# Layer 1's in-projection by Strassen's seven block products, and output projection 0 as one stage with its weights resident

## The chip, the core and the metric

The kernel runs on one core of one Trainium2 chip. The metric is the time of one launch on the device, in microseconds, by the median of several runs. The core has a matrix engine (TensorE, here PE) and three engines that work element by element: VectorE (DVE), ScalarE (ACT) and GpSimd (POOL). SyncE (SP) issues the DMAs. Tiles lie in SBUF, 128 partitions wide; matmuls write to PSUM, from which ACT and DVE read.

## What is computed

Two layers of a small diffusion backbone, over 2176 tokens (128 of a prompt, 2048 latent), 1024 channels, float32. Layer 0 mixes with gated linear attention and a spatial gate, layer 1 with centred pooling means and a short gated convolution. The change is in layer 1's input projection (`h @ w_in_odd`, 1024 to 3072 channels) and in the order and the blocks of layer 0's output projection:

```python
def mix_odd(z, j):
    B, T, _ = z.shape
    xc, gc, xd, bd, cd, gd = split_cols(z, ODD_SPLITS)
    pooled = jnp.concatenate(
        [centred_mean(xc[..., i * DG_C:(i + 1) * DG_C], w) for i, w in enumerate(POOL_WINDOWS)],
        axis=-1) - xc
    pooled = jnp.einsum('btgc,gcd->btgd', pooled.reshape(B, T, G_C, DG_C), w_pool[j])
    o_c = pooled.reshape(B, T, BRANCH_W) * pool_scale[j] * jax.nn.silu(gc)
    u = cd * xd
    up = jnp.pad(u, ((0, 0), (1, 1), (0, 0)))
    y = up[:, :-2] * w_conv[j, 0] + up[:, 1:-1] * w_conv[j, 1] + up[:, 2:] * w_conv[j, 2]
    o_d = bd * y * jax.nn.silu(gd)
    return jnp.concatenate([o_c, o_d], axis=-1)
...
for l in range(DEPTH):
    h = rmsnorm(x, norm_g[l]) * (1.0 + scale) + shift
    ...
    out = out @ w_out[l]
    x = x + gate * out
return rmsnorm(x, final_norm_g), finals
```

## The kernel before

**Products.** Channels lie on partitions, tokens along the free dimension. Every large float32 product is made of three fp32r matmuls: both operands are split in a rounded part `hi` and a rest `lo`, and hi x hi, hi x lo and lo x hi are summed in PSUM (`mm3`, L212). `split` (L197) makes `hi` by a copy on ACT and `lo = src - hi` by a subtraction on DVE or, every third time, on POOL (`lo_engine`, L193). `gemm_ch` (L220) makes one tile of 128 output channels: it loads 128x1024 weights with `load_w` (L204; three `hi`/`lo` pairs in the pool `wp`), splits them, and for each group of at most 512 tokens issues 8 x 3 matmuls.

**Stages.** Layer 0's in-projection and mixing run to about 854 us, in blocks of 512 and 640 tokens. Then come four token blocks of 544 (`BLK2`), each with three stages: output projection 0 (`out0`, L975, through `out_proj`, L955), layer 1's in-projection and mixing (`in1`, L1002), output projection 1 with the final norm (`out1`, L1116, and `out1_last`, L1140, for the last block). The order is written out by hand in the last lines of the kernel: out0(3), out0(2), in1(3), out1(3), out0(1), in1(2), out1(2), out0(0), in1(1), out1(1), in1(0), out1(0). So the output projection 0 of a block runs one stage ahead of the in1 that needs it.

**in1.** It loads the residual stream `x1` and the row `r` of reciprocal norms from DRAM, makes the normed operand `h` for eight channel tiles (`make_t`, L348, on DVE; `make_h`, L359: `hi` on ACT, `lo` on DVE), and for each of four heads `hh` runs six `gemm_ch` calls (cd, xd, gate of D, xc, gate of C, bd), each in two groups of 268 to 276 tokens. The results are consumed from PSUM by ACT copies, DVE products and `silu_psum` (L277); pooling steps are additions on POOL (L1082).

**Side work.** Smaller work is cut into generators that `tick` (L143) advances once per `gemm_ch`. `finish_o` (L837) is such work: per tile of 128 tokens it combines the attention halves, norms them (`newton`) and splits the eight `o` tiles that `out0` reads. `finish_rstd` sums squares over the channels by matmuls with ones (L248, L249) and finishes 1/sqrt by Newton steps on ACT and DVE (L240 to L261). The code is scheduled by the framework: instructions of one engine run in the order it settles on, which may put an instruction ahead of one that the code issues earlier.

## Time and profile before

| quantity | value |
|---|---|
| median of 3 runs | 1907.23 us (1899.83 to 1910.7) |
| profiled execution, its own time | 1902.82 us |
| its span in the profile | 1901.0 us |
| mean granted TensorE clock | 0.979 |
| PE busy | 1801.7 us (95%), 16303 matmuls |
| DVE, ACT, POOL busy | 60%, 45%, 38% |

The span is the profiled execution from its first to its last recorded instruction. Busy time is the union of an engine's instructions; matmuls overlap in the engine, so the mean duration of one (290 ns) is not what it takes from the stream: that is the distance from one start to the next. A duration on DVE and POOL includes whatever the instruction waited after it had started. The name `ps_g L217` stands for any product of `mm3`; `L199` for any `lo` part, `L198` for any `hi` part.

### The profile page before, as it was taken

To read this page: it belongs to the slowest core of one execution; us is meant where nothing else is said; L and a number is where in the kernel's file an instruction comes from. 1 tells how busy PE (TensorE), PEld (TensorE's weight loads), DVE (VectorE), ACT (ScalarE), POOL (GpSimd) and SP (SyncE) were. 2 spreads that over 40 slices of the span, in tenths; PEclk is the share of its full clock that TensorE was granted. 3 is DMA by queue.
4 is the path that set the end of the run, shared out by engine and by line. 5 is a ranking of instruction groups with operands and counts; after the bars stand their busy time and mean duration, and the time that the engine had idled before them with its cause. 6 is when DMAs were issued, how large, how long until landed. Compare 5 with 4: busy or idle time off the path is not lost. (4 is left out here: it accounts for less than half of the span.)

```text
span 1901.0 us, 40150 instructions
## 1 busy us (share of the span) xinstructions
PE 1801.7 (95%) x16303; PEld 1678.6 (88%) x16303; DVE 1149.6 (60%) x2069; ACT 857.3 (45%) x1678; POOL 730.5 (38%) x707
## 2 busy tenths in 40 slices
...
GB/s 310 117 123 152 153 102 136 128 159 113 140 126 102 114 106 94 142 172 183 245 200 157 109 146 109 246 157 96 95 130 203 196 81 87 115 141 130 80 89 60
DMA packets 136121, 263.43 MB, mean 139 GB/s; under 512 B 24192, under 2 KB 60160, under 8 KB 135936
## 3 DMA queue, kind: packets, MB, share of 16 engines
...
q8 instruction: 128, 2.10, 0.5%
q14 instruction: 57, 0.47, 0.1%
...
## 5 line engine op out<-in xcount | busy, mean ns | idle before, releaser
L217 PE MATMUL ps_g<-ring_hh,wp_hi 128*128 128x272 f32 (+5 forms) x2168 | 679.1, 314 | 4.4 <-ACT ring_hh L365 2.7
L217 PE MATMUL ps_g<-ring_hl,wp_hi 128*128 128x272 f32 (+5 forms) x2168 | 672.4, 310 | 1.1 <-DVE ring_hl L366 1.0
L217 PE MATMUL ps_g<-ring_hh,wp_lo 128*128 128x272 f32 (+5 forms) x2168 | 673.1, 311 | 0.0
L198 ACT ACTIVATE wp_hi<-wp_raw 128x1024 fp32r<-128x1024 f32 (+1 forms) x256 | 271.1, 1059 | 435.5 <-PE ps_g L217 323.5
L217 PEld LDWEIGHTS ps_g<-ring_hh,wp_hi 128*128 128x128 f32 x2168 | 409.6, 189 | 27.6 <-issue 3.8
L217 PEld LDWEIGHTS ps_g<-ring_hl,wp_hi 128*128 128x128 f32 x2168 | 410.0, 189 | 18.4 <-DVE ring_hl L366 2.0
L217 PEld LDWEIGHTS ps_g<-ring_hh,wp_lo 128*128 128x128 f32 x2168 | 409.1, 189 | 16.4 <-issue 0.7
L199 DVE TENSOR_TENSOR wp_lo<-wp_raw,wp_hi 128x1024 fp32r<-128x1024 f32 (+1 forms) x174 | 226.7, 1303 | 201.2 <-ACT wp_hi L198 200.9
L199 POOL TENSOR_TENSOR wp_lo<-wp_raw,wp_hi 128x1024 fp32r<-128x1024 f32 (+1 forms) x82 | 201.1, 2452 | 362.1 <-ACT wp_hi L198 359.5
L270 POOL TENSOR_TENSOR tmp_acc<-tmp_acc,tmp_px 128x544 f32<-128x544 f32 (+4 forms) x76 | 120.4, 1584 | 160.6 <-ACT tmp_px L269 155.2
L217 PE MATMUL ps_g<-wp_hi,ring_hh 128*128 128x256 f32 (+1 forms) x528 | 157.4, 300 | 7.9 <-ACT gl_v L700 4.4
L217 PE MATMUL ps_g<-oA_oh,wp_hi 128*128 128x272 f32 (+1 forms) x512 | 149.0, 295 | 7.1 <-ACT oA_oh L198 4.0
L524 POOL TENSOR_TENSOR gl_Z<-gl_Z 128x128 f32<-128x128 f32 x170 | 91.9, 561 | 161.8 <-DVE gl_Z L524 110.6
L217 PE MATMUL ps_g<-wp_hi,ring_hl 128*128 128x256 f32 (+1 forms) x528 | 152.4, 291 | 0.5 <-DVE ring_hl L366 0.4
L217 PE MATMUL ps_g<-wp_lo,ring_hh 128*128 128x256 f32 (+1 forms) x528 | 152.6, 291 | 0.2 <-POOL wp_lo L199 0.2
L217 PE MATMUL ps_g<-oA_ol,wp_hi 128*128 128x272 f32 (+1 forms) x512 | 150.0, 294 | 2.2 <-DVE oA_ol L199 2.0
L217 PE MATMUL ps_g<-oA_oh,wp_lo 128*128 128x272 f32 (+1 forms) x512 | 149.8, 294 | 0.1
L217 PE MATMUL ps_g<-oB_oh,wp_hi 128*128 128x272 f32 (+1 forms) x512 | 147.2, 289 | 0.7 <-ACT oB_oh L198 0.7
L217 PE MATMUL ps_g<-oB_oh,wp_lo 128*128 128x272 f32 (+1 forms) x512 | 147.5, 289 | 0.0
L217 PE MATMUL ps_g<-oB_ol,wp_hi 128*128 128x272 f32 (+1 forms) x512 | 147.3, 288 | 0.0
L286 POOL TENSOR_TENSOR tmp_ev<-tmp_ev,tmp_ev 128x272 f32<-128x272 f32 (+5 forms) x52 | 51.7, 994 | 186.4 <-ACT tmp_ev L275 176.7
L508 ACT ACTIVATE gl_L<-gl_Z 128x256 f32<-128x256 f32 x204 | 81.9, 417 | 87.3 <-DVE gl_Z L524 65.5
...
## 6 DMA issues: line engine op xcount, KB each, us to landing
...
xs_y<-in_xT_dram SPq DMA_DIRECT2D x32, 272.0 KB, 3.7
dr_x<-xs_y SPq DMA_DIRECT2D x32, 272.0 KB, 3.4
...
```

Of the source, the lines that this page charges most:

```text
L198: act(out=hi, in_=src, func=AF.Copy)
L199: (eng or lo_engine()).tensor_tensor(out=lo, in0=src, in1=hi.bitcast(F32), op=ALU.subtract)
L217: mm(out=out, lhsT=a, rhs=b, start=start and i == 0, stop=stop and i == n - 1)
L270: eng.tensor_tensor(out=acc, in0=acc, in1=sq, op=ALU.add)
L286: eng.tensor_tensor(out=x, in0=x, in1=s, op=ALU.mult)
L508: act(out=dst.rearrange("p (b t s) -> p t b s", t=2, s=s), in_=diag_ap(Z, 2 * i, s), func=AF.Exp, scale=1.0 / 16.0)
L524: (dve if i >= 2 or s < 4 else gps).tensor_tensor(out=dst, in0=dst, in1=bc(src), op=ALU.add)
```

## The change

**Output projection 0 as one stage.** It works in five blocks of its own (`BLKO`: 512, 512, 512, 384 and 256 tokens, from the end), one group per channel tile. Its eight weight tiles are split once, in the first block, and kept (three in `wp`, five in a new pool `wr`). While block i is multiplied, `finish_o` of block i+1 is ticked along. All five blocks run ahead of layer 1; the last `finish_rstd` is called at once, and the pools of this part are closed before layer 1's are opened in their place.

**In-projection by pairs.** The 24 output tiles of a block form 12 pairs, and the 8 channel tiles are halved into 4 + 4, the tokens into two parts of 272 or 280 columns. With A the weights of a pair (2 x 2 blocks) and B the operand (2 x 2 blocks), each pair takes seven products instead of eight: A11 B11, A12 B21, S1 T1, S2 T2, S3 T3, A22 T4, S4 B22, where S1 to S4 are sums of weight blocks and T1 to T4 sums of operand blocks. Several products add up in the same PSUM bank; ACT copies intermediate sums out (`copy`), and DVE makes the final sums (`plus`). `operand` prepares for each of four k the seven B matrices in `hi` and `lo`, on DVE, POOL and ACT. Weights are now loaded in halves of 128x512 (7 raw, 5 `hi` and 5 `lo` buffers); POOL takes three `lo` parts of seven. Block 3, which comes first, makes S1 to S4 (two additions each on POOL and DVE) and stores them in DRAM; blocks 2, 1 and 0 load them.

**Output projection 1** is as before, in weight halves, with two early parts placed at the end of in1 (`fill`).

```diff
+BLKO = [(1664, 2176), (1152, 1664), (640, 1152), (256, 640), (0, 256)]
+NBO = len(BLKO)
...
+    def w_out0(c):
+        if c == len(wres):
+            if c < NHI:
+                wres.append(load_w(wo[0, c], KT * P))
+            else:
+                raw = raw_tile()[:, 0:KT * P]
+                load(out=raw, in_=wo[0, c])
+                hi, lo = (wr.tile([P, KT * P], F32R, tag=f"{z}{c}") for z in "hl")
+                split(raw, hi, lo)
+                wres.append((hi, lo))
...
+    for i in range(NBO):
+        f = fin_o(i + 1, 1) if i + 1 < NBO else None
+        out0(i, of)
+        of = f() if f else None
+    drain()
+    s2.close()
+    late.close()
+    sw.close()
...
+    def split_half(raw):
+
+        half_ctr[0] += 1
+        hi, lo = (wh.tile([P, 512], F32R, tag=z, bufs=5) for z in ("hi", "lo"))
+        split(raw, hi, lo, gps if half_ctr[0] % 7 in (1, 3, 5) else dve)
+        return hi, lo
...
+        def sums(self):
+            R = self.raw
+            for i, (a, b, op, eng) in enumerate((("A21", "A22", ALU.add, gps),
+                                                 ("S1", "A11", ALU.subtract, dve),
+                                                 ("A11", "A21", ALU.subtract, gps),
+                                                 ("A12", "S2", ALU.subtract, dve))):
+                t = R[f"S{i + 1}"] = raw_half()
+                eng.tensor_tensor(out=t, in0=R[a], in1=R[b], op=op)
+                load(out=d_s[self.i][i], in_=t)
+
+        def get(self, name):
+            if name not in self.raw:
+                self.raw[name] = raw_half(d_s[self.i][int(name[1]) - 1] if name[0] == "S"
+                                          else self.src(name))
+            return split_half(self.raw[name])
...
+        for k in range(4):
+            h = []
+            for kk in (k, k + 4):
+                x = xk_tile(w)
+                load(out=x, in_=d_x1[kk][:, c0:c0 + w])
...
+            t = {n: ring.tile([P, 2, JW], F32R, tag="t", bufs=28) for n in B}
+            hi = {n: z[:, 0, 0:jw] for n, z in t.items()}
+            lo = {n: z[:, 1, 0:jw] for n, z in t.items()}
+            raw = {n: tmp.tile([P, JW], F32, tag="T", bufs=3)[:, 0:jw] for n in ("T1", "T2", "T3", "T4")}
+            b11, b12 = (h[0][:, a:a + jw] for a in (0, HALF))
+            b21, b22 = (h[1][:, a:a + jw] for a in (0, HALF))
+            for n, z, e in (("B11", b11, dve), ("B21", b21, gps), ("B22", b22, dve)):
+                split(z, hi[n], lo[n], e)
+            for n, x, y, e in (("T1", b12, b11, gps), ("T2", b22, raw["T1"], dve),
+                               ("T3", b22, b12, gps), ("T4", b21, raw["T2"], dve)):
+                e.tensor_tensor(out=raw[n], in0=x, in1=y, op=ALU.subtract)
+            for n, e in (("T1", dve), ("T2", gps), ("T3", dve), ("T4", gps)):
+                split(raw[n], hi[n], lo[n], e)
+            for n in B:
+                B[n].append((hi[n], lo[n]))
...
+        def plus(dst, x, y):
+            dve.tensor_tensor(out=dst, in0=x, in1=y, op=ALU.add)
...
+        class Pair:
+            def __init__(self, i):
+                self.w = Weights(i, last)
+                self.j, self.m, self.c11, self.c22, self.c21, self.c12 = makers[i](i // 3)
+
+            def mul(self, bank, a, b, start):
+                mm3(bank[:, 0:self.m], half_pairs(self.w.get(a), [
+                    tuple(z[:, self.j:self.j + self.m] for z in t) for t in B[b]]), start=start,
+                    resumed=not start)
+
+            def copy(self):
+                z = tmp.tile([P, JW], F32, tag="U", bufs=4)[:, 0:self.m]
+                act(out=z, in_=self.P[:, 0:self.m], func=AF.Copy)
+                return z
+
+            def m1(self):
+                self.P = gtile()
+                self.mul(self.P, "A11", "B11", True)
+                self.M = self.copy()
+
+            def m2(self):
+                p2 = gtile()
+                self.mul(p2, "A12", "B21", True)
+                self.c11(self.M, p2[:, 0:self.m])
+
+            def m5(self):
+                self.P3 = gtile()
+                self.mul(self.P3, "S1", "T1", True)
+
+            def m6(self):
+                self.mul(self.P, "S2", "T2", False)
+                self.U = self.copy()
+
+            def m7(self):
+                self.mul(self.P, "S3", "T3", False)
+                self.c22(self.copy(), self.P3[:, 0:self.m])
+
+            def m4(self):
+                self.mul(self.P, "A22", "T4", False)
+                self.c21(self.P[:, 0:self.m])
+
+            def m3(self):
+                self.mul(self.P3, "S4", "B22", False)
+                self.c12(self.P3[:, 0:self.m], self.U)
...
+        old_p = None
+        for i in range(len(PAIRS) + 1):
+            p = Pair(i) if i < len(PAIRS) else None
+            if p:
+                if last:
+                    p.w.load("A11", "A12", "A21")
+                p.m1()
+            if old_p:
+                old_p.m7()
+            if p:
+                p.m2()
+            else:
+                fill(0)
+            if old_p:
+                old_p.m4()
+                tick()
+                old_p.m3()
+            if p:
+                if last:
+                    p.w.load("A22")
+                    p.w.sums()
+                p.m5()
+                p.m6()
+                tick()
+            old_p = p
+
+    def block(bi):
         t0, t1 = range1(bi)
...
+    for bi in reversed(range(NB2)):
+        block(bi)
```

The framework settles the order on each engine. On PE, before, the last products of out0(2) (`ps_g_11728`, operands `oB`) are followed by the first of in1(3) (operands `ring_h`):

```order
L217 MATMUL ps_g_11728<-oB_oh_11207,wp_hi_11698 128x272
L217 MATMUL ps_g_11728<-oB_ol_11208,wp_hi_11698 128x272
L217 MATMUL ps_g_11728<-oB_oh_11207,wp_lo_11699 128x272
L217 MATMUL ps_g_11824<-ring_hh_11763,wp_hi_11820 128x272
L217 MATMUL ps_g_11824<-ring_hl_11764,wp_hi_11820 128x272
L217 MATMUL ps_g_11824<-ring_hh_11763,wp_lo_11821 128x272
```

After, this is the end of the fifth block of output projection 0 (`ps_g_12520`), then the two sums of its `finish_rstd`, then layer 1 (`ring_t` are the B matrices, `wh` the weight halves):

```order
L225 MATMUL ps_g_12520<-oA_oh_12264,wr_h_9_10821 128x256
L225 MATMUL ps_g_12520<-oA_ol_12265,wr_h_9_10821 128x256
L225 MATMUL ps_g_12520<-oA_oh_12264,wr_l_10_10822 128x256
L257 MATMUL ps_s_12552<-tmp_nw_12553,cst_ones_r_75 128x256
L258 MATMUL ps_s_12552<-tmp_nw_12554,cst_ones_r_75 128x256
L225 MATMUL ps_g_12795<-ring_t_12645,wh_hi_12796 128x272 x2
L225 MATMUL ps_g_12795<-ring_t_12645,wh_lo_12797 128x272
L225 MATMUL ps_g_12814<-ring_t_12646,wh_hi_12815 128x272
L225 MATMUL ps_g_12846<-ring_t_12647,wh_hi_12847 128x272
L225 MATMUL ps_g_12890<-ring_t_12645,wh_hi_12891 128x272 x2
```

What stood beside other products now stands behind the last sums; the first products of layer 1 advance together, k by k.

On SP, before, the loads of `x1` for in1(3) (`ring_xk`) and of `r` stand among the loads and stores of out0(2):

```order
L962 DMA xs_y_11630<-in_xT_dram 128x544
L985 DMA dr_r_176<-tmp_r_50_11336 128x544
L980 DMA dr_x_3_81_180<-xs_y_11438 128x544
L1022 DMA tmp_r_11758<-dr_r_176 128x544
L206 DMA wp_raw_11818<-in_w_dram 128x1024
L962 DMA xs_y_11694<-in_xT_dram 128x544
L1026 DMA ring_xk_11774<-dr_x_2_80_179 128x544
L980 DMA dr_x_4_82_181<-xs_y_11502 128x544
L1026 DMA ring_xk_11781<-dr_x_3_81_180 128x544
```

After, they stand behind the store of the last `r` (from `tmp_r_12551`):

```order
L1456 DMA yp_ys_15147<-dr_x_6_84_183 128x536
L1456 DMA yp_ys_15216<-dr_x_7_85_184 128x536
L990 DMA dr_r_176<-tmp_r_143_12551 128x256
L1109 DMA ring_xk_12637<-dr_x_0_78_177 128x544
L1109 DMA ring_xk_12641<-dr_x_4_82_181 128x544
L1109 DMA ring_xk_12674<-dr_x_1_79_178 128x544
L1109 DMA ring_xk_12678<-dr_x_5_83_182 128x544
L1109 DMA ring_xk_12711<-dr_x_2_80_179 128x544
```

All eight loads are behind an instruction that waits for the last Newton step.

On DVE, in the in-projection, before, steps that read PSUM (`ps_g`) and the conv steps (L1060, L1063) alternate with the `lo` part of 1024 columns of weights (L199):

```order
L1054 TENSOR_TENSOR tmp_ev_12413<-ps_g_12447,tmp_ev_12326 128x272
L199 TENSOR_TENSOR oB_ol_11881<-f_o_12230,oB_oh_11880 128x128
L1060 TENSOR_SCALAR tmp_ev_12474<-tmp_ev_12413,xs_wcv_10415 128x536
L1063 SCALAR_TENSOR_TENSOR tmp_ev_12474<-tmp_ev_12413,xs_wcv_10415,tmp_ev_12474 128x536
L199 TENSOR_TENSOR wp_lo_12646<-wp_raw_12643,wp_hi_12645 128x1024
L1063 SCALAR_TENSOR_TENSOR tmp_ev_12474<-tmp_ev_12413,xs_wcv_10415,tmp_ev_12474 128x536
L280 TENSOR_SCALAR tmp_ev_12478<-ps_g_12485 128x268
L280 TENSOR_SCALAR tmp_ev_12478<-ps_g_12516 128x268
```

After, in block 3, between the sums from PSUM (L1183) and the mixing steps stand `lo` parts of 512 columns (L206) and the weight sums (L1076):

```order
L1183 TENSOR_TENSOR tmp_ev_13363<-tmp_U_13389,ps_g_13410 128x272
L1076 TENSOR_TENSOR wh_raw_13473<-wh_raw_13470,wh_raw_13366 128x512
L1183 TENSOR_TENSOR tmp_s_13196<-tmp_U_13407,ps_g_13328 128x272
L1076 TENSOR_TENSOR wh_raw_13479<-wh_raw_13368,wh_raw_13473 128x512
L206 TENSOR_TENSOR wh_lo_13500<-wh_raw_13473,wh_hi_13499 128x512
L1202 TENSOR_TENSOR tmp_ev_13194<-ps_g_13203,tmp_ev_13193 128x272
L1183 TENSOR_TENSOR tmp_ev_13193<-ps_g_13328,tmp_U_13361 128x272
L206 TENSOR_TENSOR wh_lo_13545<-wh_raw_13476,wh_hi_13544 128x512
L206 TENSOR_TENSOR wh_lo_13566<-wh_raw_13521,wh_hi_13565 128x512
L1214 TENSOR_SCALAR tmp_ev_13464<-tmp_ev_13194,c_wcv_12602 128x536
L206 TENSOR_TENSOR wh_lo_13605<-wh_raw_13479,wh_hi_13604 128x512
L1217 SCALAR_TENSOR_TENSOR tmp_ev_13464<-tmp_ev_13194,c_wcv_12602,tmp_ev_13464 128x536 x2
```

In this stretch, six of twelve rows read two SBUF operands that belong to the weights (L206, L1076); before, one of eight does (L199).

## Rows read from the trace of the kernel before

**Rows 1.** Page, part 1: busy us (share of the span) and instructions of each engine.

```profile
PE 1801.7 (95%) x16303; PEld 1678.6 (88%) x16303; DVE 1149.6 (60%) x2069; ACT 857.3 (45%) x1678; POOL 730.5 (38%) x707
```

**Rows 2.** Busy time in windows of layer 1; after PE: PEld, DVE, ACT, POOL, clock, DMA, GB/s.

```profile
950.00:1067.00 117.00, 115.13 (x907) 113.78 (x906) 78.05 (x122) 56.08 (x110) 50.64 (x46) 1.00 0.55 169
1163.00:1277.00 114.00, 112.76 (x891) 111.86 (x890) 75.11 (x102) 49.87 (x90) 44.13 (x33) 1.00 0.56 182
```

**Rows 3.** PE by line and form, 950 to 1880 us: count, busy us, mean ns.

```profile
L217 PE MATMUL ps_g<-ring_hh,wp_hi 128*128 128x272 f32 x1152 | 333.6, 290 | 2.7 <-ACT ring_hh L365 2.7
L217 PE MATMUL ps_g<-ring_hh,wp_hi 128*128 128x276 f32 x192 | 55.8, 291 | 0.0
```

**Rows 4.** Timeline of PE in two undisturbed stretches: start, duration, what.

```profile
120.14 0.39 PE L217 MATMUL ps_g<-ring_hl,wp_hi 128*128 128x512 f32 x1
124.22 0.39 PE L217 MATMUL ps_g<-ring_hl,wp_hi 128*128 128x512 f32 x1
...
1399.73 0.29 PE L217 MATMUL ps_g<-oA_oh,wp_hi 128*128 128x272 f32 x1
1403.98 0.29 PE L217 MATMUL ps_g<-oA_ol,wp_hi 128*128 128x272 f32 x1
```

**Rows 5.** Timeline of PE, first matmul of output projection 0, with its wait.

```profile
854.21 0.52 PE L217 MATMUL ps_g<-oA_oh,wp_hi 128*128 128x272 f32 x2 [3.96 <-ACT oA_oh L198]
```

**Rows 6.** Busy time in four slices of output projection 0, columns as in rows 2.

```profile
850.00:860.00 10.00, 6.04 (x37) 5.84 (x36) 3.92 (x8) 4.41 (x14) 4.65 (x6) 0.83 0.65 202
870.00:880.00 10.00, 7.96 (x50) 7.73 (x50) 9.13 (x17) 4.64 (x12) 3.83 (x4) 0.83 0.54 156
890.00:900.00 10.00, 6.54 (x48) 5.82 (x46) 8.28 (x16) 3.10 (x9) 4.71 (x6) 0.97 0.69 218
900.00:910.00 10.00, 7.79 (x45) 7.17 (x46) 7.02 (x9) 6.78 (x15) 6.45 (x6) 0.69 0.89 280
```

**Rows 7.** Timeline of ACT and DVE, first and last Newton step of a `finish_rstd`.

```profile
1452.24 0.49 ACT L240 ACTIVATE tmp_nw<-ps_s,cst_eps 128x272 f32<-128x272 f32 x1 [0.24 <-PE ps_s L249]
1454.75 0.44 DVE L261 SCALAR_TENSOR_TENSOR tmp_r<-tmp_nw,tmp_nw 128x272 f32<-128x272 f32 x1
```

**Rows 8.** DMA issues, 854 to 1901 us: count, KB, median us to landing.

```profile
ring_xk<-dr_x SPq DMA_DIRECT2D x8, 272.0 KB, 3.6
```

**Rows 9.** Timeline of DVE and POOL in two places where they meet.

```profile
1461.21 1.22 DVE L199 TENSOR_TENSOR wp_lo<-wp_raw,wp_hi 128x1024 fp32r<-128x1024 f32 x1
1462.34 4.76 DVE L366 SCALAR_TENSOR_TENSOR ring_hl<-ring_xk,cst_ada,ring_hh 128x560 fp32r<-128x560 f32 x2
1463.78 2.72 POOL L199 TENSOR_TENSOR wp_lo<-wp_raw,wp_hi 128x1024 fp32r<-128x1024 f32 x1
...
1626.53 2.92 DVE L1089 SCALAR_TENSOR_TENSOR tmp_ev<-tmp_ev,tmp_ev 128x544 f32<-128x544 f32 x1 [4.84 <-POOL tmp_ev L1082]
1626.47 2.40 POOL L199 TENSOR_TENSOR wp_lo<-wp_raw,wp_hi 128x1024 fp32r<-128x1024 f32 x1
```

**Rows 10.** DVE and POOL by line and form, 830 to 1901 us, columns as in rows 3.

```profile
L199 DVE TENSOR_TENSOR wp_lo<-wp_raw,wp_hi 128x1024 fp32r<-128x1024 f32 x110 | 141.2, 1284 | 127.3 <-ACT wp_hi L198 127.1
L366 DVE SCALAR_TENSOR_TENSOR ring_hl<-ring_xk,cst_ada,ring_hh 128x560 fp32r<-128x560 f32 x16 | 21.3, 1340 | 3.0 <-ACT ring_hh L365 2.9
...
L965 DVE SCALAR_TENSOR_TENSOR xs_y<-ps_g,cst_ada,xs_y 128x272 f32<-128x272 f32 x56 | 26.9, 492 | 21.6 <-PE ps_g L217 20.5 <-DMA dr_x<-xs_y 1.1
L1063 DVE SCALAR_TENSOR_TENSOR tmp_ev<-tmp_ev,xs_wcv,tmp_ev 128x544 f32<-128x544 f32 x16 | 16.6, 1038 | 0.1
L366 DVE SCALAR_TENSOR_TENSOR ring_hl<-ring_xk,cst_ada,ring_hh 128x544 fp32r<-128x544 f32 x8 | 6.1, 778 | 0.3
...
L199 POOL TENSOR_TENSOR wp_lo<-wp_raw,wp_hi 128x1024 fp32r<-128x1024 f32 x50 | 121.9, 2438 | 188.4 <-ACT wp_hi L198 188.1
L1069 POOL TENSOR_TENSOR tmp_ev<-tmp_ev,tmp_ev 128x544 f32<-128x544 f32 x8 | 11.0, 1378 | 0.4
L286 POOL TENSOR_TENSOR tmp_ev<-tmp_ev,tmp_ev 128x272 f32<-128x272 f32 x16 | 12.8, 802 | 51.8 <-ACT tmp_ev L275 46.9 <-DVE wp_lo L199 4.9
```

471 lines of the change are left out of this document (292 added, 179 removed).

## Prediction

> **What bounds the kernel now.** I read the page's busy shares first: PE is busy 95% of the 1901.0 us, DVE 60%, ACT 45%, POOL 38% [rows 1]. Then the stages of layer 1, by windows: in the in-projections, with the interleaved pieces of the other block, PE is busy 115.13 of 117 and 112.76 of 114 us [rows 2]. Its idle stretches lie in output projection 0, around 854, 870 and 900 us [rows 5, 6]. So PE's matmuls are the time; DVE and POOL run in their shadow, with 78.05 and 50.64 us of 117 in the fullest stage. The question is whether the change, which takes matmuls away and gives DVE, POOL and ACT more to do, leaves it so. The sum is made on the profiled run, 1902.82 us (1901.0 of span, 1.8 around it), which is 4.4 under the median, 1907.23; about 0.5% (9.5 us) is what a measurement here tells from no change.
>
> **The change part by part.**
>
> *In-projection, fewer products.* Before: 1152 x 3 matmuls of 272 columns and 192 x 6 of 268 and 276, 4608 in all [rows 3]. After: 4 blocks x 12 pairs x 7 products x 12 matmuls = 4032, of which 2688 have 272 columns and 1344 have 280. The stages took 117 us for 907 matmuls and 114 for 891 [rows 2], so 0.1284 us each with all small stalls, against 0.125 from start to start in an undisturbed stretch (34 from 1399.73 to 1403.98, [rows 4]). 4608 x 0.1284 = 591.7; 2688 x 0.1284 + 1344 x 0.1284 x 280/272 = 522.8. **-69** (-67 at 0.125).
>
> *Output projection 0 in wider groups.* Before 1536 matmuls of 272. After 576 of 512, 192 of 384, 192 of 256. 512 columns go at 0.227 (18 from 120.14 to 124.22, [rows 4]); between 0.125 and 0.227 a column costs 0.00042, so 0.172 at 384 and 0.118 at 256. 1536 x 0.125 = 192.0; 130.8 + 33.0 + 22.7 = 186.5. **-5.5**.
>
> *The start of output projection 0.* Its first matmul waited 3.96 us for the last `o` tile [rows 5]. The first block now needs the tiles 13 to 16 and not the 32 columns of tile 12, which came last. **-4** (0 to -8).
>
> *Its block changes.* Before, PE idled 2.0 us of the slice from 870 and 3.5 + 2.2 of those from 890 and 900, and the granted clock fell to 0.83 and 0.69 in two of them [rows 6], some 3 us more. That 11 goes, and this comes: at the changes from the first block to the second and from the second to the third, the sums of the last heads and the next `ob` matmuls stand in PE's order with no other matmul between. Each is like the stretch at 900, 5.7 us plus 1.5 of clock. **+3** net (-5 to +12).
>
> *The new seam ahead of layer 1.* Before, the loads and the preparation of in1's operand ran beside output projection 0, whose matmuls covered them. Now the first product stands directly behind the last sums of `finish_rstd`. On SP the eight `ring_xk` loads stand behind the store of the last `r2`, and on DVE and ACT the preparation behind its Newton steps, so this is bare. From the last matmul: update 0.49 and POOL add 0.80 [rows 10], square and split on ACT 0.49 each and on DVE 0.44 [rows 7], sums 0.3, Newton 3.0 (1452.24 to 1455.19, [rows 7]): 6.0. Then a load, 3.6 [rows 8]. Then preparation of four k: on DVE each k has two 544-column steps and six of 272, 2 x 0.78 + 6 x 0.44 = 4.2, together 16.8; POOL has five of 272 each, 5 x 0.78 = 3.9 (802 ns in [rows 10]), 15.6 together. Side by side 17, one after the other 32. Some 48 matmuls (6 us) fit in between, since the first four products advance k by k. 9.6 + (17 to 32) - 6 = 21 to 36; I take **+27**, nearer the lower end because the ops with no partner at POOL run free, and **+2** for the clock after it (the slice with the 4 us wait had 0.83, [rows 6]).
>
> *DVE and POOL in the in-projection.* Here the trace shows what decides. The step L1089 on DVE took 2.92 us where it overlaps POOL's `wp_lo` of 2.40, and ended just after it; two L366 took 4.76 together, over POOL's 1.45 and 2.72 [rows 9]; L366 at 544 columns with POOL quiet means 778 ns, at 560 columns 1340 [rows 10]. A DVE step with two inputs in SBUF waits while POOL does a two-input step. Steps that read PSUM don't show it: L965 keeps to 492 ns over 56 of them [rows 10].
>
> The Trainium skill, "SBUF — State Buffer", section "Who interferes with whom", says the same more strictly: a DVE instruction with two SBUF inputs and a GpSimd instruction that reads SBUF exclude each other for the whole instruction. By that rule the third block's heads below would need 15.4 + 25.3 us of the shared port, 36 us more than PE's time over four heads instead of my 19, and the sum would be 1906.
>
> One head after the change is 252 matmuls, 31.7 us of PE. Its DVE work: 12 `lo` of 512 columns at 0.73 (778 ns at 544), 5 steps of 544 at 0.78 and 4 of 272 at 0.44, all with two SBUF inputs, 14.5 us; 14 that read PSUM at 0.44 and three single ones, 7.3. Together 21.8 for 21 exposed steps. Its POOL work: 9 `lo` of 512 at 1.22 (half of 2438 ns), 2 steps of 544 and on average 2.5 pooling steps of like width at 1.38, one of 272 at 0.80: 18.0. In the rows the exposed steps lost 0.06 us (`wp_lo`, mean 1284 ns against 1.22 us where POOL was quiet), 0.26 (L1063 against 778), 0.55 (L366), [rows 9, 10], with POOL busy 43% [rows 2]; with POOL at 57% I take 0.30, about their mean. DVE: 21.8 + 21 x 0.30 = 28.1 of 31.7. PE still leads, but at 89% the queues run dry in bursts, with only five `hi`/`lo` halves (7 us of PE) ahead: **+8** over the twelve heads of blocks 2, 1 and 0 (0 to +32).
>
> *The sums S1 to S4.* Only block 3 makes them: per head 6 on DVE (0.73) and 6 on POOL (1.22). POOL 25.3, 80% of PE's time, so I take 0.38 a step: DVE 21.8 + 4.4 + 27 x 0.38 = 36.5. That is 4.8 us over PE, in four heads: **+19** (0 to +43). From block 2 on they come from DRAM; 84 halves of 256 KB in some 127 us are 173 GB/s, under the 182 that a stage moved before [rows 2]: nothing.
>
> *From out1 to the next in1.* The next block's preparation stands ahead of out1's updates on DVE, so that out1's 48 us of matmuls cover it; what is bare is the like of the 2.0 us at 870. **+6** for three (0 to +18, if the first reads of `t` come late).
>
> ACT was busy 56 of 117 us [rows 2]. The 36 U copies of a block (under 0.49 each, [rows 7]) add 18, and the `hi` parts of 43008 columns of weights a block where 24576 were add about as much: some 93 of 127, so it stays off the path. out1 has 1536 matmuls before and after and changes nothing.
>
> Sum: -69 - 5.5 - 4 + 3 + 27 + 2 + 8 + 19 + 6 = **-13.5**, so 1889 on the profiled run and 1893 on the median's scale (x 1907.23/1902.82).
>
> **The rivals.**
>
> A. *Matmuls decide alone.* DVE's waits fall into its spare time, the seam is at its short end: 8 and 19 become 0, 27 becomes 20, 6 becomes 3. -50.5: 1852, 1857 by the median. For it: with DVE at 78 of 117 us PE lost only 2. Against it: block 3 has no spare time on DVE.
>
> B. *DVE becomes the bound, slower than before.* If an exposed step loses 0.6 us, as L366 did, a head costs DVE 21.8 + 12.6 = 34.4, 2.7 over PE, twelve times 32; in block 3 26.2 + 27 x 0.6 = 42.4, 10.7 over, four times 43. 75 in place of 27: 1937, 1941 by the median. It decides from the point where the loss passes (31.7 - 21.8)/21 = 0.47 us. For it: POOL's steps last 1.2 to 1.4 us, twice DVE's. Against it: the mean of the largest group, `wp_lo`, lost only 0.06. The rule of the Trainium skill's page "SBUF — State Buffer" is the mechanism of this rival.
>
> C. *The seam comes back three times.* If the `t` tiles come free only at the end of an in-projection and out1's updates hold the queues, each change costs preparation less what fits between, 17 to 32 - 6, mean 16: 48 in place of 6, 1931, 1935 by the median. Against it: in the order of DVE's instructions the preparation stands ahead of out1.
>
> **How the numbers follow.** The forecast case (1875 to 1912) has 0.37, A 0.28, B 0.20, C 0.08, and 0.07 is for what I don't see. A is faster; of the forecast case about half is faster by over 0.5%, a third within it, the rest slower; B and C are slower. That makes 0.47 faster, 0.16 within 0.5%, 0.37 slower. The range goes from A's 1857 less a few us to B's and C's 1940: 1850 to 1945. The likeliest case alone is 1875 to 1912.
>
> **What would show it.** In-projection of blocks 2, 1 and 0 at about 129 to 132 us each with PE over 95% busy, and 4032 matmuls (the -69); a PE gap of 20 to 36 us behind the last sums of output projection 0, ended by a `ring_t` tile; in block 3 an in-projection about 20 us longer than block 2's, its PE waits ended by `wh_lo` or a sum on DVE or POOL, and DVE's two-input means at 0.3 to 0.4 us above the free ones. Wrong would make it: block 3 as short as block 2 (A), DVE busy over 95% in blocks 2 to 0 with PE under 90% (B), gaps of 10 us or more at each out1's end (C).

## The result and the profile after

The changed kernel takes **2022.45 us** (median of 4 executions, 2020.83 to 2030.98) where the kernel before took 1903.53 beside it: a ratio of 1.0633 (95% interval 1.058 to 1.0685). The forecast was 1893, the range 1850 to 1945. The sign is wrong, and the time lies outside the range. Its profiled execution has a span of 2021.4 us and a mean granted clock of 0.946 (before 1901.0 and 0.979).

Busy time by engine after, against [rows 1]:

```profile
PE 1791.8 (89%) x15115; PEld 1617.9 (80%) x15115; DVE 1380.5 (68%) x2360; ACT 988.5 (49%) x2008; POOL 968.7 (48%) x923
```

PE issues 1188 matmuls fewer (1152 of them are the change's, 576 in each of the two projections), and yet its share is 6 points lower. By windows (columns as in [rows 2]): output projection 0; the in-projection of block 3; the change from block 3's output projection 1 to block 2's in-projection; that in-projection; its end; the in-projections of blocks 1 and 0.

```profile
850.00:1090.00 240.00, 219.82 (x1100) 187.53 (x1099) 136.00 (x214) 99.12 (x204) 117.11 (x98) 0.94 0.54 167
...
1106.00:1306.00 200.00, 157.57 (x982) 144.88 (x983) 166.53 (x200) 90.23 (x188) 138.13 (x115) 0.87 0.39 129
...
1375.00:1405.00 30.00, 30.00 (x240) 30.00 (x239) 16.42 (x28) 17.52 (x35) 15.00 (x16) 1.00 0.51 146
1382.00:1521.00 139.00, 129.14 (x976) 126.89 (x975) 108.72 (x155) 79.35 (x160) 82.34 (x74) 0.98 0.61 187
1520.00:1549.00 29.00, 18.67 (x106) 17.18 (x106) 25.41 (x34) 15.79 (x36) 20.63 (x18) 0.71 0.35 108
...
1598.00:1732.00 134.00, 127.89 (x985) 125.82 (x984) 107.36 (x155) 79.03 (x160) 80.98 (x73) 1.00 0.59 189
1805.00:1946.00 141.00, 131.79 (x984) 129.92 (x984) 107.51 (x191) 78.81 (x153) 76.26 (x75) 0.98 0.53 165
```

PE was busy 115.13 of 117 us in [rows 2]. Now it loses 42 us in block 3, 6 to 10 in each later in-projection and 10 of 29 at the end of one; the granted clock is lowest where PE idles most. It loses nothing at the change from output projection 1 to the next in-projection (30.00 of 30.00 us). What PE waits for from 840 us on (us in total, times, the longest):

```profile
PE ps_g L225 <- DVE wh_lo L206: 27.5, 26, 5.0
PE ps_g L225 <- ACT wh_hi L205: 25.8, 13, 4.6
PE ps_s L1287 <- DVE tmp_ev L1272: 19.5, 6, 8.3
PE ps_g L225 <- ACT ring_t L205: 12.5, 4, 11.0
```

The first row is the `lo` halves, the second the `hi` halves (18.9 of the 25.8 us in block 3), the third the end of each in-projection (L1287 multiplies the last head's pooled means), the fourth the seam ahead of layer 1.

**The seam**, in the timelines of PE, SP and DVE, and as a window:

```profile
1094.30 0.39 PE L257 MATMUL ps_s<-tmp_nw,cst_ones_r 128*128 128x256 f32 x1 [4.18 <-ACT tmp_nw L205]
1106.31 0.59 PE L225 MATMUL ps_g<-ring_t,wh_hi 128*128 128x272 f32 x1 [10.97 <-ACT ring_t L205]
...
1092.93 3.80 SPq L1456 DMA_DIRECT2D yp_ys<-dr_x  x7
1097.69 0.32 SPq L990 DMA_DIRECT2D dr_r<-tmp_r  x1
1098.06 11.03 SPq L1109 DMA_DIRECT2D ring_xk<-dr_x  x4
...
1103.67 2.18 DVE L359 SCALAR_TENSOR_TENSOR ring_xk<-ring_xk,cst_gs,tmp_r 128x544 f32<-128x544 f32 x3 [6.00 <-DMA ring_xk<-dr_x]
...
1090.00:1132.00 42.00, 19.04 (x66) 14.61 (x64) 27.00 (x42) 20.75 (x48) 22.86 (x26) 0.60 0.51 167
```

The forecast chain is there: sums, Newton, store of `r` at 1097.69, and only then the loads of `ring_xk`. Something that the forecast did not price stands with them: seven loads of `yp_ys` (one more at 1091.88), which output projection 1 reads over 200 us later, were issued just ahead on the same queue.

**The end of an in-projection**, block 2's, on DVE, on POOL and on PE:

```profile
1534.85 1.50 DVE L206 TENSOR_TENSOR ring_t<-ring_xk,ring_t 128x280 fp32r<-128x280 f32 x1
1536.28 1.02 DVE L206 TENSOR_TENSOR ring_t<-tmp_T,ring_t 128x280 fp32r<-128x280 f32 x1
1537.34 0.92 DVE L1124 TENSOR_TENSOR tmp_T<-ring_xk,tmp_T 128x280 f32<-128x280 f32 x1
1538.18 1.82 DVE L206 TENSOR_TENSOR wh_lo<-wh_raw,wh_hi 128x512 fp32r<-128x512 f32 x1
1539.93 1.01 DVE L206 TENSOR_TENSOR ring_t<-tmp_T,ring_t 128x280 fp32r<-128x280 f32 x1
1540.86 1.02 DVE L206 TENSOR_TENSOR ring_t<-ring_xk,ring_t 128x280 fp32r<-128x280 f32 x1
1541.81 0.71 DVE L1272 SCALAR_TENSOR_TENSOR tmp_ev<-tmp_ev,tmp_ev 128x544 f32<-128x544 f32 x1
...
1534.31 1.74 POOL L206 TENSOR_TENSOR wh_lo<-wh_raw,wh_hi 128x512 fp32r<-128x512 f32 x1
...
1537.91 1.54 POOL L1265 TENSOR_TENSOR tmp_ev<-tmp_ev 128x545 f32<-128x545 f32 x1
...
1536.10 0.59 PE L225 MATMUL ps_g<-o_oh,wh_lo 128*128 128x272 f32 x1 [3.46 <-POOL wh_lo L206]
...
1537.18 0.43 PE L225 MATMUL ps_g<-o_oh,wh_hi 128*128 128x272 f32 x1
1537.40 0.43 PE L225 MATMUL ps_g<-o_ol,wh_hi 128*128 128x272 f32 x1
1537.63 0.43 PE L225 MATMUL ps_g<-o_oh,wh_lo 128*128 128x272 f32 x1
1542.58 2.18 PE L1287 MATMUL ps_s<-tmp_ev,c_wpl 128*128 128x272 f32 x4 [4.52 <-DVE tmp_ev L1272]
```

`ring_t` and `tmp_T` are the *next* block's operand. The scheduler drew its preparation so far forward that the last head's own step L1272 queues behind it, one of 0.9 to 1.8 us after another, and PE stands. The starts on PE tell of the clock too: 0.22 from one 272-column matmul to the next, against 0.125 in [rows 4]. The granted clock is 1.00 from 1520 to 1531 us and 0.50 from 1532 to 1548, the lower of its two levels (1.2 GHz against 2.4); before it fell PE had idled 2.35 us, and the holes of 3.46 and 4.52 lie in the stretch at the lower level.

DVE and POOL by form, 1106 to 1960 us (count, busy us, mean ns), against [rows 10]:

```profile
L206 DVE TENSOR_TENSOR wh_lo<-wh_raw,wh_hi 128x512 fp32r<-128x512 f32 x220 | 222.9, 1020 | 65.0 <-ACT wh_hi L205 62.3
...
L206 POOL TENSOR_TENSOR wh_lo<-wh_raw,wh_hi 128x512 fp32r<-128x512 f32 x164 | 234.8, 1433 | 178.1 <-ACT wh_hi L205 168.3 <-PE ps_g L225 4.2 <-DMA wh_raw<-dr_s 3.7
```

With POOL idle, a `wh_lo` on DVE took 0.68 us, so the mean step lost 0.34 us. The mean hides two kinds. Of the 228 in the whole trace 123 took 0.70 us or less; each of the 105 others ended 0.54 to 0.56 us behind the end of a two-input POOL step, whenever it had started. The fence on block 2's end shows it: POOL's step from 1537.91 ends at 1539.45, DVE's `wh_lo` from 1538.18 at 1540.00. Such a step waited until POOL's was nearly done.

### The profile page after: what moved, and what is told of

Its sections match the earlier page's. It is cut to its first block, busy times and chain, and to the rows that moved or that the text cites. A ratio compares the mean times of both kernels' runs of the same rounds, so it can differ in the third digit from the quotient of the medians.

```text
span 2021.4 us, 39668 instructions
## 1 busy us (share of the span) xinstructions
PE 1791.8 (89%) x15115; PEld 1617.9 (80%) x15115; DVE 1380.5 (68%) x2360; ACT 988.5 (49%) x2008; POOL 968.7 (48%) x923
## 5 line engine op out<-in xcount | busy, mean ns | idle before, releaser
L225 PE MATMUL ps_g<-ring_t,wh_hi 128*128 128x272 f32 (+1 forms) x2688 | 543.7, 302 | 50.9 <-ACT wh_hi L205 18.9
L225 PEld LDWEIGHTS ps_g<-ring_t,wh_hi 128*128 128x128 f32 x2688 | 442.2, 198 | 62.5 <-ACT wh_hi L205 22.2
L225 PE MATMUL ps_g<-ring_t,wh_lo 128*128 128x272 f32 (+1 forms) x1344 | 396.5, 302 | 25.7 <-DVE wh_lo L206 22.5
L205 ACT ACTIVATE wh_hi<-wh_raw 128x512 fp32r<-128x512 f32 x400 | 246.6, 627 | 301.2 <-PE ps_g L225 205.9
L206 POOL TENSOR_TENSOR wh_lo<-wh_raw,wh_hi 128x512 fp32r<-128x512 f32 x172 | 245.6, 1429 | 192.1 <-ACT wh_hi L205 182.2
L225 PEld LDWEIGHTS ps_g<-ring_t,wh_lo 128*128 128x128 f32 x1344 | 262.3, 198 | 32.7 <-DVE wh_lo L206 28.0
L206 DVE TENSOR_TENSOR wh_lo<-wh_raw,wh_hi 128x512 fp32r<-128x512 f32 x228 | 230.9, 1019 | 68.8 <-ACT wh_hi L205 66.0
L225 PE MATMUL ps_g<-ring_hh,wp_hi 128*128 128x512 f32 (+2 forms) x632 | 234.4, 371 | 5.3 <-DVE tmp_ev L782 3.2
L225 PE MATMUL ps_g<-ring_hl,wp_hi 128*128 128x512 f32 (+2 forms) x632 | 230.5, 365 | 0.0
L206 POOL TENSOR_TENSOR wp_lo<-wp_raw,wp_hi 128x1024 fp32r<-128x1024 f32 (+1 forms) x31 | 76.6, 2470 | 173.6 <-ACT wp_hi L205 170.9
L206 DVE TENSOR_TENSOR wp_lo<-wp_raw,wp_hi 128x1024 fp32r<-128x1024 f32 (+1 forms) x68 | 88.6, 1303 | 80.1 <-ACT wp_hi L205 79.4
L225 PEld LDWEIGHTS ps_g<-ring_hh,wp_hi 128*128 128x128 f32 x632 | 120.9, 191 | 27.0 <-issue 3.6
```

Of the source, the lines that this page charges most:

```text
L205: act(out=hi, in_=src, func=AF.Copy)
L206: (eng or lo_engine()).tensor_tensor(out=lo, in0=src, in1=hi.bitcast(F32), op=ALU.subtract)
L225: mm(out=out, lhsT=a, rhs=b, start=start and i == 0, stop=stop and i == n - 1, skip_group_check=resumed)
```

## The experiments

Theory 1: the forecast's own mechanisms, mis-sized: DVE and POOL shut each other out (the largest, worth 40 to 80 us), the sums S1 to S4, and preparation in the way of the last head. Theory 2, the rival: the product form is not the trouble; running output projection 0 as one stage is, since its alternation with the in-projections had covered every change of stage. Runs named with one time are single executions; executions of one kernel scatter by some 5 us either way, so no verdict is built on less.

**The change's first half alone: `x_old_in1`.** Output projection 0 as after, with its wider groups and resident weights, in-projection and output projection 1 as before.

```diff
+    for i in range(NBO):
+        f = fin_o(i + 1, 1) if i + 1 < NBO else None
+        out0(i, of)
...
-    out0(3, o3)
-    out0(2, g2())
...
     out1(3, run(in1(3), 4))
-    out0(1, f())
```

> The change's first half alone: output projection 0 in its five blocks with resident weights ahead of everything, then in1 and out1 as they were before (no Strassen products). Theory 1 (the Strassen part with its work on DVE and POOL is what costs): output projection 0 up to 1090 us as after, a bare seam of about 20, then four in1 and out1 at the old rate, 790, and the tail, 17: span about 1917, 0.5 to 1.5% over before. Theory 2 (the one stage and its seam are the main loss): 1950 or more.

Measured 1976.14 (ratio 1.0369, 1.0333 to 1.0406). PE at its first change of block, then windows of the seam and of the three changes:

```profile
1315.47 0.59 PE L257 MATMUL ps_s<-tmp_nw,cst_ones_r 128*128 128x268 f32 x1 [2.93 <-ACT tmp_nw L205]
...
1329.31 0.59 PE L225 MATMUL ps_g<-ring_hl,wp_hi 128*128 128x272 f32 x1 [8.83 <-DVE ring_hl L375]
...
1091.00:1120.00 29.00, 13.65 (x62) 11.96 (x61) 11.17 (x18) 6.94 (x12) 1.49 (x3) 0.65 0.58 188
1305.00:1345.00 40.00, 21.36 (x134) 18.71 (x132) 22.33 (x33) 11.08 (x18) 4.41 (x4) 0.79 0.38 133
1528.00:1570.00 42.00, 23.29 (x141) 20.88 (x140) 23.53 (x34) 11.17 (x18) 4.44 (x4) 0.76 0.39 129
1754.00:1790.00 36.00, 36.00 (x288) 36.00 (x287) 22.02 (x31) 14.06 (x27) 11.62 (x14) 1.00 0.49 167
```

For this kernel the rival holds: the first half alone costs some 74 us. At 0.128 a matmul, about 21 are lost at the seam (idle 9.46 us at 1104.24) and about 47 at two changes of block, which an output projection 0 had covered before; the third, which had no such cover before either, loses nothing, and some 6 are left for output projection 0 (240 us as after). The changed kernel shares only part of this: the seam and output projection 0 are there, but at its changes of block PE is never idle, since the next operand is prepared early (1375 to 1405 us above; 1592 to 1622 and 1800 to 1830 likewise). So some 47 of the 74 us are not in its loss.

**DVE and POOL: `x_no_lo`, `x_pool_one`, `x_lo_dve`.** The first uses the `hi` halves of in1's and out1's weights in the place of `lo`; the second makes POOL's `lo` from one input (raw x 2^-12, not the rest); the third gives POOL's `lo` halves to DVE, whose load grows.

```diff
-        split(raw, hi, lo, gps if half_ctr[0] % 7 in (1, 3, 5) else dve)
+        act(out=hi, in_=raw, func=AF.Copy); lo = hi                  # x_no_lo
+        gps.tensor_scalar(out=lo, in0=raw, scalar1=2.0 ** -12, ...)   # x_pool_one, in POOL's turns
+        split(raw, hi, lo, dve)                                       # x_lo_dve
```

> Layer 1's weight halves keep only their rounded part: the 400 subtractions that make the lo halves are left out, and the products read the hi half in their place, so PE's matmuls are as many as after. Theory 1 (DVE and POOL cannot deliver the halves): the in-projections of blocks 2, 1, 0 fall from about 150 to 132 to 136 us, block 3's from about 230 to 170, the stalls at the ends shrink too; the whole about 1890 to 1910. Theory 3 (it is the short supply of five hi buffers and the chain behind ACT, not DVE and POOL): under 40 us saved, 1980 or more.

> The lo halves that POOL makes (three of seven) become an operation with one input, raw times a constant, in place of raw minus hi; the values are not the rests any more, count and size stay. Theory 1 in its form of exclusion (a two-input step on DVE waits while POOL does a two-input step): DVE's wh_lo falls from a mean of 1019 ns to 750 to 800, and 40 to 80 us go from the whole. Theory 1 in its form of mere load (too many steps): DVE's mean stays near 1000 and under 15 us go.

> All lo halves of weights on DVE, none on POOL. Theory 1 as exclusion: POOL's share falls by 9 steps of 1.43 us a head and DVE's wh_lo returns to 0.70 to 0.75, so DVE's 9 more steps cost it 6.5 us a head but save it as much waiting; the in-projections get shorter or stay, 1980 to 2020. Theory 1 as load (DVE at 80% has no room): blocks 2 to 0 take 10 us more each, 2040 or more.

Measured 1925.26, 1980.62 and 1971.95. Block 3 and block 2 of `x_no_lo`, by windows:

```profile
1110.00:1269.00 159.00, 140.25 (x984) 132.76 (x985) 99.08 (x157) 87.77 (x189) 79.43 (x80) 0.92 0.51 165
1338.00:1464.00 126.00, 126.00 (x985) 125.53 (x984) 56.32 (x113) 81.12 (x163) 30.96 (x41) 1.00 0.67 207
```

The 97 us that go are 15 to 35 fewer than theory 1 expected. Without `lo` halves PE is never idle in block 2's in-projection: 985 matmuls in 126 us, 0.128 each. That is the forecast's price of the products, and what block 2's in-projection took above it, 14 us, is waiting, with some loss of clock. The `wh_lo` of `x_pool_one` on DVE, with one DVE step inside a step of POOL; the `wh_lo` of `x_lo_dve`, and its block 2:

```profile
L1042 DVE TENSOR_TENSOR wh_lo<-wh_raw,wh_hi 128x512 fp32r<-128x512 f32 x226 | 194.0, 865 | 96.1 <-ACT wh_hi L1038 91.9 <-issue 0.5 <-POOL wh_lo L1040 0.4
...
1856.39 0.68 DVE L1042 TENSOR_TENSOR wh_lo<-wh_raw,wh_hi 128x512 fp32r<-128x512 f32 x1
...
1855.77 1.50 POOL L1040 TENSOR_SCALAR wh_lo<-wh_raw 128x512 fp32r<-128x512 f32 x1
```

```profile
L206 DVE TENSOR_TENSOR wh_lo<-wh_raw,wh_hi 128x512 fp32r<-128x512 f32 x395 | 329.5, 846 | 67.8 <-ACT wh_hi L205 62.0 <-DMA wh_raw<-in_w_dram 1.6
...
1357.00:1490.00 133.00, 129.08 (x992) 127.93 (x991) 114.06 (x191) 82.15 (x164) 37.33 (x41) 0.99 0.62 195
```

Taking POOL's second input away shortens DVE's step by 0.15 us (expected were 0.22 to 0.27) although POOL's own grows to 1617 ns, and gains 42 us. Of 57 DVE steps that met only the one-input step 39 took 0.70 us or less; the 18 others, all but one begun within half a microsecond behind its start, took 0.74 to 1.10 and still ended before it did. The 42 us are not all exclusion: POOL's step no longer reads `hi`, so it no longer waits for ACT either, and no run separates the two. With some 170 steps more on DVE the kernel gains 50, more than the expected range allowed. Of these about 23 lie in block 3 and 28 in the other three; their in-projections alone gain 20. Block 2's 972 matmuls take 133.0 us (140.9 after), and DVE is busy 114.06 us for 992 matmuls, where it was 108.72 for 976: 36 more `lo` steps, 24 us at 0.68 each, add 5. So POOL's help costs more than it brings, and DVE's load is not what holds these stages.

**The sums: `x_no_sums`.** Plain weight blocks stand in the place of S1 to S4, which are not made.

```diff
-                    p.w.sums()
```

> S1 to S4 are left out everywhere: the four products read a plain weight block each in their place (A21, A11, A22, A12), loaded like the others; nothing is stored. Theory 1: block 3's in-projection falls from about 230 us to the 150 of block 2 plus what the seam's preparation costs, so 40 to 60 us go in block 3 alone, and blocks 2 to 0 stay. If the sums are hidden: under 10.

Measured 1975.95, 46 less. Block 3's in-projection, by windows:

```profile
1106.00:1258.00 152.00, 136.97 (x983) 130.96 (x984) 124.96 (x176) 90.53 (x187) 98.04 (x92) 0.93 0.48 153
```

152 us in the place of 200. Load is only a part: in the changed kernel's block 3 ACT waits for the sums one after the other (S1 on POOL, then S2 and S4 on DVE, each before its `hi`), and for weight halves that land late. Its two longest waits there, and below them the one on the sums in `x_best` (under *All together*), where POOL makes all four:

```profile
ACT wh_hi L205 <- DVE wh_raw L1076: 28.4, 10, 4.4
ACT wh_hi L205 <- DMA wh_raw<-in_w_dram: 20.8, 9, 4.1
...
ACT wh_hi L205 <- POOL wh_raw L1077: 21.5, 19, 3.0
```

**The hoisted preparation: `x_late_prep`.** One tiny DVE step ties the first load of the next block's operand behind the last two `o` tiles.

```diff
         r = tmp.tile([P, 560], F32, tag="r", bufs=1)[:, 0:w]
+        if prev_o8:
+            dve.tensor_tensor(out=r[:, 0:1], in0=prev_o8[3][1][:, 0:1].bitcast(F32),
+                              in1=prev_o8[7][1][:, 0:1].bitcast(F32), op=ALU.add)
         load(out=r, in_=d_r[:, c0:c0 + w])
```

> After, with one tiny addition: the next block's r tile is first written from the last two o tiles of this block, so that the preparation of the next operand cannot start ahead of the last head's consumers. Theory 4 (the preparation, hoisted into the end of the in-projection, keeps DVE from the last head's chain and opens the hole ahead of out1): the holes of 15 to 26 us at the three changes shrink to 5 to 8, 30 to 60 us go from the whole, 1960 to 1990. If the holes are the bare length of that chain: under 10 us go.

Measured 1986.58, 36 less. PE's wait of 19.5 us for L1272 is all but gone (the lines lie four lower in this kernel):

```profile
PE ps_s L1291 <- DVE tmp_ev L1276: 0.3, 1, 0.3
```

`x_late_dve` joins it to `x_lo_dve`:

> Both edits: the late preparation, and all lo halves of weights on DVE. If both theories 1 (exclusion) and 4 hold the gains add up: 1930 to 1970. If DVE is simply full, it is no better than the late preparation alone.

Measured 1936.37: 86 less, the sum of the two.

**The tiles of output projection 0: `x_per2`.** `finish_o` of the next block advances two steps a tick.

```diff
-        f = fin_o(i + 1, 1) if i + 1 < NBO else None
+        f = fin_o(i + 1, 1, 2) if i + 1 < NBO else None
```

> In output projection 0 the side work finish_o runs two steps a tick, so that the next block's o tiles are asked for in the first half of a block and not by its end. Theory 5 (the 40 us lost in that stage are late o tiles): the stalls at the first two changes of block shrink by more than half and the stage takes 220 to 225 us in place of 239. If DVE and POOL are the limit there, or the DMAs: 235 or more.

Measured 2002.13, 20 less, and the stage ends at 1070, not 1090:

```profile
850.00:1070.00 220.00, 212.67 (x1102) 184.76 (x1101) 137.10 (x212) 98.96 (x203) 115.05 (x98) 0.98 0.58 178
```

PE idles 7 of 220 us in the place of 20 of 240. The `o` tiles came late: with one stage a block's tiles must be finished beside the previous block, some 44 us (192 matmuls at 0.227).

**All together: `x_best`, `x_best_fin`.** `x_best` has the late preparation, all `lo` halves on DVE, two steps of `finish_o` a tick, and the sums on POOL alone; `x_best_fin` also stores the last `r` from ACT's queue and spreads the final scaling L1486 over ticks.

> Four edits together: late preparation, all lo halves of weights on DVE, two steps of finish_o a tick, and all of S1 to S4 on POOL (which the third edit left idle) in place of two on each engine. If the gains measured so far add (36 + 50 + 20) the first three give 1916; the sums on POOL free 4.4 us of DVE a head in block 3, where DVE is full: 10 to 20 more, 1895 to 1906. If DVE is not what block 3 waits for: 1915 or more.

> The same with two more edits. The store of the last r of output projection 0 goes out on ACT's queue, so that the ring_xk loads on SP do not stand behind it: the bare seam, 16 us to its first matmul, should shrink by the Newton steps that it no longer waits for, 4 to 7. And the eight final products of a block (L1486, 6.6 us of DVE in one piece, behind which a lo half stood for 5 us) are issued one a tick: 3 to 5 us a block, 10 to 14. Together 1880 to 1890 if the four edits give 1900; if DVE fills the space at once, no change.

Measured 1920.19 and 1914.33. Block 3 and block 2 of `x_best_fin`:

```profile
1087.00:1261.00 174.00, 146.63 (x984) 136.66 (x984) 152.66 (x200) 83.42 (x174) 116.12 (x96) 0.90 0.41 145
1320.00:1454.00 134.00, 128.41 (x990) 126.34 (x989) 116.10 (x195) 80.66 (x159) 33.04 (x38) 1.00 0.62 199
```

Neither reaches the gain hoped for. If they add, the first three edits alone give 1916, so the sums on POOL gain nothing: it is the other case of that expectation (1915 or more), in which DVE is not what block 3 waits for, and the row of ACT above shows the wait moved to POOL. The two further edits gain 6 us, within the scatter. Block 3 (174 us) and the seam (16.8) stay.

**The sums elsewhere: `x_presum`, `x_presum_b`.** S1 to S4 are made on DVE beside output projection 0; the second also has six `hi`/`lo` halves, and five raw buffers in the place of seven.

```diff
+        if i == 1:
+            side(presums(), 1)      # per pair: 2 loads, 4 additions on DVE in place, 4 stores
-        hi, lo = (wh.tile([P, 512], F32R, tag=z, bufs=5) for z in ("hi", "lo"))
+        hi, lo = (wh.tile([P, 512], F32R, tag=z, bufs=6) for z in ("hi", "lo"))   # x_presum_b
```

> x_best_fin with the sums S1 to S4 of all twelve pairs taken out of block 3's in-projection: they are made on DVE as side work of output projection 0 (from its second block on, one pair every two ticks, in place in the raw weight tiles that are free there). If the sums are what lengthens block 3's in-projection (about 174 us against 135 in x_best_fin, although they had been moved to POOL), it falls to 135 to 140, and the 48 additions (35 us at 0.73) disappear in the stage from 960 to 1070 us, in which DVE is busy 52%: 1914 - 37 = 1877 (1870 to 1890), under the kernel before by 1%. Rival: block 3 is long for another reason (the queues still full of preparation after the seam, the clock), then it stays over 160 and the time over 1900; or the additions delay finish_o's tiles on DVE, then the stage of output projection 0 grows by 10 to 35 from its 219 us and the time is 1890 to 1912.

> x_presum with six hi/lo weight halves in place of five (and five raw buffers in place of seven, which pays for the room). PE waited 30 us for a lo half on DVE in x_best_fin, in 28 pieces. If those are bursts in DVE's queue, a sixth half, 1.5 us of matmuls more ahead, takes a third to a half of them: 10 to 15 us under x_presum. If DVE's rate is the limit in the in-projections (93% busy there), or the loads now come late with fewer raw buffers, nothing: within 4 us of x_presum, or slower.

Measured 1915.55 (1.0094, 1.0075 to 1.0112) and 1915.7 (1.0087). Output projection 0 and block 3 of `x_presum`:

```profile
850.00:1093.00 243.00, 218.75 (x1088) 186.28 (x1087) 175.03 (x255) 94.81 (x196) 111.48 (x93) 0.96 0.81 257
1113.00:1256.00 143.00, 134.59 (x980) 130.43 (x981) 122.27 (x203) 87.59 (x178) 44.80 (x52) 0.92 0.51 160
```

Block 3 gains 31 us, a little under what was expected, and output projection 0 gives 23 back, as the expectation's rival had it, though DVE is busy only 72% of it: the additions stand in the queue of the `o` tiles, and the DMA share rises from 0.56 (`x_best_fin`) to 0.81. The sixth half, with two raw buffers fewer, gains nothing.

**The seam: `x_seam2`, `x_ys`, `x_seam3`.** `x_seam2` puts the last `finish_rstd` into layer 1; `x_ys` ties the loads of `yp_ys` behind an `o` tile; `x_seam3` does both.

```diff
-            fin()
+            load(out=d_acc, in_=acc)          # finished a few pairs into block 3 (x_seam2, x_seam3)
+            dve.tensor_tensor(out=y[:, 0:1], in0=o8[1][1][:, 0:1].bitcast(F32), ...)   # x_ys, x_seam3
             load(out=y, in_=d_x1[c][:, t0:t1])
```

> x_best_fin with the last finish_rstd of output projection 0 put off: its sum of squares goes to DRAM, and the matmuls with ones, the Newton steps and the store of r run as side work of layer 1, a few pairs into block 3 (only block 0 reads that r, 600 us later). By the order of steps: the hole ahead of the sums (5.5 us at 1075.54) and its two small ones go, and the hole ahead of the first product shrinks since nothing stands ahead of the preparation: 31 us become 10 to 18, 1914 - 13 to 21 = 1893 to 1901. By the room in SBUF: the preparation still begins only when the last matmuls of output projection 0 have ended, so the one hole becomes about as long as the two together less the sums' own 1 us: 25 to 30, 1908 to 1913.

> x_best_fin (1914) with one more edit: the eight loads of ys for output projection 1 are tied behind an o tile of the same block (one small DVE step ahead of each), so that they no longer stand ahead of the ring_xk loads on SP at the seam. If these loads hold the seam (they were issued from 1072.43 to 1077.8, the first ring_xk at 1078.51), the first product starts 5 to 8 us earlier after the last one of output projection 0: 1906 to 1910. If the last finish_rstd holds it, nothing: 1912 to 1916.

> x_seam2 (hole of 17.1 us) with the same edit. Now nothing but the last store of output projection 0 stands ahead of the ring_xk loads: load 3.6, four steps of preparation 2.5 to 3: a hole of 6 to 9 us, 8 to 11 us under x_seam2's 1924, 1913 to 1916; if SBUF room holds the loads until the last matmul has ended, 9 to 12 us of hole.

Measured 1924.02, 1915.14 and 1916.1. From the last matmul of output projection 0 to the first product: 16.8 us in `x_best_fin`, 17.1 in `x_seam2`, 11.7 in `x_ys`, 12.3 in `x_seam3`. In the changed kernel it was 16.2. So the order of `finish_rstd` was not the point, and neither was the store of `r`, which all four have out of the way of these loads; 5 us of the hole were the loads of `yp_ys`. That room in SBUF holds the loads back is not excluded: 12.3 is nearer to that case of the expectation (9 to 12) than to the other (6 to 9). The 5 us do not show in the time: `x_ys` is where `x_best_fin` was (1914.33), and `x_seam2` is 10 over it, outside both of its expected ranges, with block 3's in-projection 3 us longer; the rest was not taken apart. What is left in `x_seam3` is a late load and the first steps:

```profile
1077.39 1.40 SPq L1122 DMA_DIRECT2D ring_xk<-dr_x  x3
...
1081.55 2.17 DVE L359 SCALAR_TENSOR_TENSOR ring_xk<-ring_xk,cst_gs,tmp_r 128x544 f32<-128x544 f32 x3 [5.92 <-DMA ring_xk<-dr_x]
```

The sums beside it, in the last two or three blocks of output projection 0 (`x_seam2_sums3`, `x_seam2_sums2`) or from the second on (`x_seam3_sums`):

> x_seam2 with the sums S1 to S4 made on DVE beside the last two blocks (384 and 256 tokens, about 60 us) of output projection 0, one pair every two ticks, the rest drained behind it. If finish_o was what the sums disturbed: block 3's in-projection is 143 as in x_presum (-31), the stage grows by what does not fit: 48 additions at 0.8 are 38 us on an engine that is about half free there, so 5 to 15 longer: 16 to 26 under x_seam2. If the sums hold the preparation at the seam instead: the seam is 20 us longer and the gain is about 0 to 10.

> The same from the third block on (512, 384 and 256 tokens, some 110 us). The finish_o of two blocks is still beside it. If finish_o is what suffers, between x_presum's growth of 24 us and none: 10 to 25 under x_seam2; against x_seam2_sums3 the drained rest at the seam is gone. The one of the two that is faster tells which of the two neighbours is the dearer.

> x_seam3 with the sums S1 to S4 beside output projection 0 from its second block on, as in x_presum. x_presum gained 31 us in block 3 and lost 24 in output projection 0 and some more at the seam, where its queues were fuller. With the seam free of the ys loads the net is -5 to -10: 1903 to 1910; if the additions crowd DVE in output projection 0 as before, no difference from x_seam3.

Measured 1924.41, 1919.55 and 1914.91 (1.006, 1.0038 to 1.0082): each time block 3 falls to 143 to 146 us and output projection 0 grows to 243 to 250. None gains what was hoped for (16 to 26, 10 to 25 and 5 to 10 us). No version beats the kernel before; the best are 0.6 to 0.9% over it.

## Why the prediction was wrong

Four terms of the sum failed, each far too small: the tiles at output projection 0's block changes (+3), the preparation that was taken as covered (+6), the `lo` halves (+8) and the sums (+19). One size came out right with a wrong make-up, the seam.

**Right: the products.** 4032 matmuls instead of 4608, 0.128 each where nothing else holds PE (`x_no_lo`). The -69 is there and is eaten elsewhere. The case of rival A (matmuls decide alone) did not come about. Output projection 0 began at 851.01 us without its wait (854.21 before), 3.2 of the 4 us forecast.

**Right in size, in part by luck: the seam.** +29 with its clock. From 1090 to 1132 us PE made 66 matmuls in 42 us, so about 33 were lost: 23 of idle (two holes of 4.18 and 10.97 us and smaller ones) where 27 was taken, and some 10 by the clock where 2 was. The gap of 20 to 36 us that was to show it is not there. Nor was the named chain what made the hole, 16.2 us from the last matmul to the first product: it was 16.8 when the store of `r` no longer stood ahead of the loads, and at 17.1 when the whole last `finish_rstd` did not. The `yp_ys` loads on SP were missed.

**Wrong: "Its block changes ... +3".** The step looked only at the sums of squares at the changes, and not at the tiles that the next block needs; these had one block's time to be made in. `x_per2` shows 20 us there.

**Wrong: "so that out1's 48 us of matmuls cover it; ... +6".** The preparation does stand ahead of out1's updates, as the order showed. But it stands ahead of the last head's chain too, and out1 needs the `o` tiles of that chain. `x_late_prep` measures 36. The cover itself is as forecast: at the changes PE is never idle. The same fact was counted only where it helps. Rival C named these places and gave them 48, by another mechanism.

**Wrong: "+8 over the twelve heads".** The loss per step was nearly right: 0.34 us on the mean where 0.30 was taken. What failed is the step from there to PE, that PE leads while DVE's share is under 100%: in block 2 DVE was busy 108.72 of 139 us, and PE still lost 9.9 of them. `x_lo_dve` measures what the `lo` halves on POOL cost: 20 us in the in-projections of blocks 2 to 0, 28 with their other stages, and about 23 more in block 3. The in-projections took 140.9, 134.8 and 141.9 us where 129 to 132 was forecast. Rival B had the mechanism, but its condition, 0.47 us a step, was not met. Nor does DVE's share decide: in `x_lo_dve` it was higher, 114.06 of 133 us, and PE lost only 3.9. A `lo` half passes through ACT and then POOL or DVE, and PE takes one every 1.5 us (12 matmuls of 0.125); that single late halves, and not a full engine, stop PE is argued from this, not shown by a run of its own.

The Trainium skill, "SBUF — State Buffer", section "Who interferes with whom", states the mechanism of that rival: a DVE instruction with two SBUF inputs contends with a GpSimd instruction that reads SBUF. The trace agrees (1020 ns with POOL's `lo` halves, 846 without; all 105 long steps end 0.54 to 0.56 us behind a two-input POOL step), but not in full for POOL's one-input step, which reads SBUF too: 39 of 57 DVE steps beside it were not longer. The prediction's sum by that rule has a slip: a head of block 3 has 14.5 + 4.4 = 18.9 us of such DVE steps by its own terms, not 15.4, which makes 50 in the place of 36 and 1920 in the place of 1906.

**Wrong: the sums, +19.** 46. They were priced as load on DVE and POOL; the rows of ACT above show a chain of waits from engine to engine, and for late weight halves, as well. Moving all sums to POOL gained nothing.

Added to the forecast: 17 for the tiles, 30 for the preparation, 42 for POOL's `lo` halves, 27 for the sums: 116 over -13.5 gives +103, of +119 measured. The sum is a rough one: about 23 of the 50 us of `x_lo_dve` lie in block 3, beside the 46 of the sums, and counted once they leave +80. So 16 to 39 us were not taken apart. The fall of the clock is contained in each term.

What the forecast lacked as a case is what `x_old_in1` shows: the alternation of stages in the kernel before was itself the cover, and giving it up costs 74 us when nothing else is done. The changed kernel covers its changes of block by early preparation, and pays for that at the ends of its in-projections.

What stays open: why the additions cost output projection 0 nearly as much as they free in block 3, with DVE at 72%; DMA share and queue order both changed at once.
